# Weights and activations at other places in their buffers, in the second half of a decoder step

## The chip, the cores and the metric

The kernel runs on one core of a Trainium2 chip. The metric is the device time of one execution in microseconds (us). The engines that matter are TensorE (PE in the profile: matmuls; PEld: the loads of its stationary operand, which overlap the matmuls), ScalarE (ACT), VectorE (DVE), GpSimd (POOL) and SyncE (SP, which issues the DMAs).

## The reference

One layer of a hybrid decoder is computed for 288 tokens at once: 256 of a prompt and 8 times 4 of a sample group, all in float32.

```
h = RMSNorm(x); P = h @ w_in            # conv branch, attention branch, memory branch, gates
x = x + (g_A*y_A + g_B*y_B + g_M*y_M) @ w_o
x = x + relu(RMSNorm(x) @ w_up)^2 @ w_down
```

`D_MODEL` is 2048 and the hidden width of the feed-forward part is 8192. The last two lines are the part of the kernel that the change touches: the output projection `w_o`, and the feed-forward part `w_up`, `w_down`.

## The kernel before

All activations lie transposed in SBUF: 128 features in the partitions, 288 tokens along the free axis. A float32 product is made of three fast ones. Both operands are split in a high part (a cast to float32r) and a low part (what the cast left over), and high*high, high*low and low*high are summed in PSUM.

**Weights** arrive in 504 slabs of 128 x 1024 floats, eight blocks of 128 x 128 side by side. SP loads a slab into one of four `wr` buffers (`load_slab`, L285). ACT casts it into a `wh` buffer (`cast_weights`, L303), DVE subtracts and writes the low part to a `wl` buffer (`sub_part`, L314). There are four `wh` and four `wl` buffers.

**Matmuls.** `main_tile` makes one output tile of 128 features x 288 tokens from two slabs; `products` issues 24 matmuls for each slab, all through `chunk` (L486): sixteen with blocks of `wh` as the stationary operand, and the high and low activations in turn as the moving one, then eight with blocks of `wl` and the high activations. Every one of these 24 loads new weights (128 columns) and streams 288 columns.

**Places.** The split activations of the first half, and `h2`, which feeds `w_up`, are `Acts`: two `a` buffers of 320 floats, used from float `AHEAD` = 12 on. The merged branches, which feed `w_o`, and the squared hidden tiles, which feed `w_down`, are `Home`s: places in the `k4` and `s` buffers, which are free by then (`make_homes`). Three of them lie in one `k4` buffer, 320 floats apart, one in an `s` buffer, each also 12 floats in. In the built program all `wr`, `wh`, `wl`, `a`, `k4` and `s` buffers start 96 bytes past a multiple of 256 bytes, so the weights of these matmuls start at 96 and the activations at 144 past such a multiple.

**Order.** All instructions are put in order when the program is built: `Order.run` keeps a list of jobs with estimated costs and pool counts, and takes the one that can start first. Tiles come from pools that turn round; a pool's size is known to this planner. For the second half, `main` issues 16 tiles of `w_o` (32 slabs), and then, four times, 16 tiles of `w_up` and 16 of `w_down` (64 slabs each time): 288 slabs in all, the last ones of the 504.

Of the kernel before, what the change touches and what calls it, by code (L numbers as in the profile page):

```python
# [8 lines left out]
F32R = mybir.dt.float32r  # L9
# [5 lines left out]
P = 128  # L15
D_MODEL = 2048
KT = D_MODEL // P
# [4 lines left out]
T = NP + NS  # L22
# [13 lines left out]
SLAB = 8 * P  # L36
N_SLABS = 504
# [37 lines left out]
class Order:  # L75
# [15 lines left out]
    def add(self, gen, rank, at=None):  # L91
        job = Job(gen, rank, self.now.ready if at is None and self.now else at or 0.0)
        self.jobs.append(job)
        was, self.now = self.now, job
        self.step(job)
        self.now = was
# [10 lines left out]
    def give(self, pool, n=1):  # L107
        self.pools[pool] += [self.now.ready] * n
# [45 lines left out]
def dve(n, *flags, **take):  # L154
    return Ask("DVE", 0.18 + n / 920.0, flags, **take)


def act(n, *flags, **take):
    return Ask("ACT", 0.22 + n / 1200.0, flags, **take)


def pool(n, *flags, **take):
    return Ask("POOL", 0.3 + n / 420.0, flags, **take)


def pe(us, *flags, **take):
    return Ask("PE", us, flags, **take)


def sp(*flags, **take):  # L170
    return Ask("SP", 0.45, flags, **take)


APART = 320
AHEAD = 12
VISIT, VISIT_K = 4, 8
MM = 0.131
MM_MEM = 0.226
# [3 lines left out]
def tile_decoder_step(ctx: ExitStack, tc: tile.TileContext, xT, memT, wall, cvec, kmat, ptab,  # L182
# [1 line left out]
                      yT, oK, oV, oCp, oCs, oMK, oMV):  # L184
    nc = tc.nc
    PS = bass.MemoryType.PSUM
    bufs = {"wr": 4, "w": 4, "a": 75, "t": 11, "k4": 9, "s": 8, "pm": 4, "pa": 3, "pl": 1}

    def open_pool(name, n, space=None):
        if space is None:  # L190
# [17 lines left out]
    def tl(p, shape, dt=F32):  # L208
        cnt[0] += 1
        return pools[p].tile(shape, dt, tag=p, name=f"{p}_{cnt[0]}")  # L210

    def bank(p):
        return tl(p, [P, 512])
# [57 lines left out]
    class Slab:  # L271
        def __init__(self, parts):
            self.parts = parts
            self.landed = [Flag() for _ in range(parts)]
            self.split = [Flag() for _ in range(parts)]
# [4 lines left out]
    def load_slab(s, part):  # L280
# [4 lines left out]
        nc.sync.dma_start(sl.raw[:, part * n:(part + 1) * n], wall[s, :, part * n:(part + 1) * n])  # L285
        sl.landed[part].at = order.landed(n * P * 4 / 1e3)

    def due(s):
        return at_slab[1] + 2.9 * (s - at_slab[0])

# [2 lines left out]
    def cast_weights():  # L293
        todo = [(0, 0), (1, 0), (0, 1), (1, 1)] + [(s, i) for s in range(2, N_SLABS) for i in range(slabs[s].parts)]
        for s, i in todo:
            sl = slabs[s]
            n = SLAB // sl.parts
            cast_at[0] = s
            yield act(n, sl.landed[i], **({} if i else {"w": 1}))
            if i == 0:  # L300
                sl.h = tl("wh", [P, SLAB], F32R)
            c = slice(i * n, (i + 1) * n)
            nc.scalar.copy(sl.h[:, c], sl.raw[:, c])  # L303
            sl.split[i].cast = order.now.ready
            add(sub_part(s, i), lambda s=s: 0 if due(s) - order.free["DVE"] < 5.0 else 4.5)

    def sub_part(s, i):
        sl = slabs[s]
        n = SLAB // sl.parts
        yield dve(n, late=Order.HOP + 0.1)  # L310
        if i == 0:
            sl.l = tl("wl", [P, SLAB], F32R)
        c = slice(i * n, (i + 1) * n)
        nc.vector.tensor_sub(sl.l[:, c], sl.raw[:, c], sl.h[:, c].bitcast(F32))  # L314
        done(sl.split[i])
        if i == sl.parts - 1:
            give("wr")
# [5 lines left out]
    class Acts:  # L323


        def __init__(self, n=T):
            c = slice(AHEAD, AHEAD + n) if n == T else slice(0, n)
            self.h, self.l = tl("a", [P, APART], F32R)[:, c], tl("a", [P, APART], F32R)[:, c]
# [178 lines left out]
    def main_tile(acts, evac, rank=1.0, n_slabs=2):  # L507
        yield pe(0.0, pm=1)
        ps = bank("pm")[:, :T]
        for i in range(n_slabs):  # L510
            slab_no[0] += 1
            yield from products(ps, FULL, acts[8 * i:8 * i + 8], i == 0, i == n_slabs - 1)
            give("w")
        add(evac(ps), rank)
# [720 lines left out]
    homes, homes_in = [], Flag()  # L1235
# [4 lines left out]

    def make_homes():
        yield sp(*conv_done, *osb_in, k4=bufs["k4"], s=bufs["s"])
        parts = []
        for _ in range(bufs["k4"]):
            x = tl("k4", [P, 1024], F32R)
            parts += [x[:, AHEAD + i * APART:AHEAD + i * APART + T] for i in range(3)]
        for _ in range(bufs["s"]):
            parts.append(tl("s", [P, 512], F32R)[:, AHEAD:AHEAD + T])
        for j in range(KT):
            homes.append(Home(parts[2 * j], parts[2 * j + 1]))  # L1250
        done(homes_in)


# [12 lines left out]
    merged = [None] * KT  # L1266

    def branch(br, j):
        def evac(ps):
            sig = gates[br, j]  # L1270
            if br == 2:
                yield dve(T, sig.flag, a=1)
                macc[j] = tl("a", [P, T])
                nc.vector.tensor_mul(macc[j], ps, sig.out)
                give("pm")
                give("t")
                return
            yield dve(T, sig.flag)
            nc.vector.tensor_mul(sig.out, ps, sig.out)
            give("pm")  # L1280
            yield dve(T)
            nc.vector.tensor_add(macc[j], macc[j], sig.out)
            give("t")
            if br == 0:
                yield act(T, homes_in)
                a = merged[j] = homes[j]
                nc.scalar.copy(a.h, macc[j])
                yield dve(T)
                nc.vector.tensor_sub(a.l, macc[j], a.h.bitcast(F32))
                give("a")  # L1290
                done(merged_in[j])
        return evac
# [41 lines left out]
        return load, evac  # L1334


    def up_tile(u, f):
        def evac(ps):
            yield dve(T, r2_done, t=1)
            r = tl("t", [P, T])  # L1340
            nc.vector.scalar_tensor_tensor(r, ps, 0.0, r2, op0=ALU.max, op1=ALU.mult)  # L1341
            give("pm")
            yield pool(T)
            nc.gpsimd.tensor_mul(r, r, r)  # L1344
            yield act(T)
            a = homes[f]
            nc.scalar.copy(a.h, r)  # L1347
            yield dve(T)
            nc.vector.tensor_sub(a.l, r, a.h.bitcast(F32))  # L1349
            give("t")  # L1350
            u[f].h, u[f].l = a.h, a.l
            done(u[f].flag)
        return evac
# [48 lines left out]
    def warm_up():  # L1402

        yield pe(4.2, pa=1)
        junk = bank("pa")
        for i in range(7):
            nc.tensor.matmul(junk, warm[:, :P], warm[:, :512], start=True, stop=True)  # L1407
        give("pa")
        give("w")

    def main():
        yield from warm_up()
        yield from mem_products()
        yield from conv_products([evac_lin(0, "pa"), evac_gat(0, "pa"), evac_lin(1, "pm"), evac_gat(1, "pm")])
        for j in range(2, CT):
            yield from main_tile(hx, evac_lin(j, "pm"))
            yield from main_tile(hx, evac_gat(j, "pm"))
        add(samples(), 3.0)
        for h in range(MH):
            yield from main_tile(hx, mem_head(h), 2 + 0.05 * h)  # L1420
        for h in range(SH):
            yield from main_tile(hx, sb_key(h), 2.2 + 0.05 * h)
            yield from main_tile(hx, sb_query(h), 2.2 + 0.05 * h)
            yield from main_tile(hx, sb_head(h), 2.2 + 0.05 * h)
        yield from branch_products(2, [Late(omem, h, om_in[h]) for h in range(MH)])
        give("a", 8)
        yield from branch_products(1, [Late(osb, h, osb_in[h]) for h in range(SH)])
        give("a", 16)
        yield from branch_products(0, [Late(cact, j, cact_flags[j]) for j in range(CT)])
        give("a", 40)  # L1430
        mg = [Late(merged, j, merged_in[j]) for j in range(KT)]
        for j in range(KT):
            load, evac = out_tile(j)
            add(load(), 2)
            yield from main_tile(mg, evac)
        add(sum_norm(sq_sum, D_MODEL, r2, r2_done, sums_2), 0.4)
        hh = [Late(h2, j, h2_in[j]) for j in range(KT)]
        for c in range(D_FF // D_MODEL):
            u = [Later() for _ in range(KT)]
            for f in range(KT):  # L1440
                yield from main_tile(hh, up_tile(u, f))
            for j in range(KT):
                yield from main_tile(u, down_tile(j, c == D_FF // D_MODEL - 1))

# [174 lines left out]
```

## Time and profile before

| what | value |
|---|---|
| time, median of 2 runs | 1639.87 us (1639.81 to 1639.92) |
| the profiled execution's own time | 1639.37 us |
| its span | 1637.6 us |
| PE busy | 1633.0 us, 12786 instructions |
| DVE busy | 992.2 us |
| ACT busy | 739.3 us |
| POOL busy | 138.9 us |
| mean DMA rate over the span | 186 GB/s |

The span runs from the first to the last instruction of the program; 1.8 us of the execution lie around it. Busy times of the engines overlap. A matmul's record lasts longer than the distance to the next one, since matmuls are pipelined: the rate of PE is read from starts and counts, not from the length of a record.

### The profile page before, as it was taken

To read this page: it belongs to the slowest core of one execution; us is meant where nothing else is said; L and a number is where in the kernel's file an instruction comes from. 1 tells how busy PE (TensorE), PEld (TensorE's weight loads), DVE (VectorE), ACT (ScalarE), POOL (GpSimd) and SP (SyncE) were. 2 spreads that over 40 slices of the span, in tenths; PEclk is the share of its full clock that TensorE was granted. 3 is DMA by queue.
4 is the path that set the end of the run, shared out by engine and by line. 5 is a ranking of instruction groups with operands and counts; after the bars stand their busy time and mean duration, and the time that the engine had idled before them with its cause. 6 is when DMAs were issued, how large, how long until landed. Compare 5 with 4: busy or idle time off the path is not lost.

```text
span 1637.6 us, 30963 instructions
## 1 busy us (share of the span) xinstructions
PE 1633.0 (100%) x12786; PEld 1615.7 (99%) x12786; DVE 992.2 (61%) x1471; ACT 739.3 (45%) x1070; POOL 138.9 (8%) x105
## 2 busy tenths in 40 slices
PE   9999999999999999999999999999999999999999
PEld 7999999999999999999999999999999999999999
DVE  8888888877777655565555544455445554455443
ACT  8746666644343534444443433333333333333332
POOL 0020000000000000001222200122001210022100
PEclk9999999999999999999999999999999999999999
DMA  9686465776755555556655555555555555555563
GB/s 339 217 184 248 148 203 195 251 257 243 256 162 167 152 184 174 169 162 202 193 175 167 170 169 173 170 168 170 167 169 168 169 173 170 169 168 168 179 192 100
DMA packets 107103, 305.39 MB, mean 186 GB/s; under 512 B 19922, under 2 KB 29522, under 8 KB 106962
## 3 DMA queue, kind: packets, MB, share of 16 engines
q1 hardware_dynamic: 106818, 303.39, 58.4%
q8 instruction: 100, 1.64, 0.4%
q14 instruction: 41, 0.34, 0.1%
q10 hardware_dynamic: 144, 0.02, 0.0%
HBM read 297.05 MB, written 6.32 MB: 185 GB/s over the span
## 4 chain that ended last, share of the span: by engine, by line
PE 100%; POOL 0%; DVE 0%; issue 0%; POOLq 0%
PE pm L486 93%; PE pm L539 3%; PE pa L486 1%; PE pl L1015 1%; PE pl L1188 0%; PE pa L852 0%; PE pa L853 0%; PE pa L851 0%; PE pl L1031 0%; PE pa L1407 0%; PE pa L825 0%; PE pa L1142 0%; PE pa L906 0%; PE pa L1139 0%; PE pa L1141 0%; PE pa L1106 0%
## 5 line engine op out<-in xcount | busy, mean ns | idle before, releaser
L303 ACT CAST wh<-wr 128x1024 fp32r<-128x1024 f32 (+1 forms) x520 | 530.5, 1023 | 652.1 <-PE pm L486 596.2
L486 PE MATMUL pm<-a,wh 128*128 128x288 f32 x5184 | 742.3, 293 | 0.0
L314 DVE TENSOR_TENSOR wl<-wr,wh 128x1024 fp32r<-128x1024 f32 (+1 forms) x520 | 616.6, 1189 | 197.2 <-ACT wh L303 192.4
L486 PEld LDWEIGHTS pm<-a,wh 128*128 128x128 f32 x5184 | 699.7, 188 | 1.3 <-issue 1.2
L486 PE MATMUL pm<-a,wl 128*128 128x288 f32 x2592 | 398.6, 293 | 0.0
L486 PEld LDWEIGHTS pm<-a,wl 128*128 128x128 f32 x2592 | 359.8, 188 | 0.0
L486 PE MATMUL pm<-k,wh 128*128 128x288 f32 x2160 | 306.8, 292 | 0.0
L486 PEld LDWEIGHTS pm<-k,wh 128*128 128x128 f32 x2160 | 290.2, 188 | 0.0
L486 PE MATMUL pm<-k,wl 128*128 128x288 f32 x1120 | 171.6, 292 | 0.0
L486 PEld LDWEIGHTS pm<-k,wl 128*128 128x128 f32 x1120 | 155.0, 188 | 0.0
L1344 POOL TENSOR_TENSOR t<-t 128x288 f32<-128x288 f32 x64 | 96.3, 1505 | 599.9 <-DVE t L1341 599.9
L1358 DVE TENSOR_TENSOR a<-a,pm 128x288 f32<-128x288 f32 x64 | 29.1, 454 | 122.5 <-PE pm L486 122.5
L1341 DVE SCALAR_TENSOR_TENSOR t<-pm,r 128x288 f32<-128x288 f32 x64 | 29.2, 458 | 90.3 <-PE pm L486 90.3
L1347 ACT CAST k<-t 128x288 fp32r<-128x288 f32 x56 | 24.2, 433 | 115.7 <-POOL t L1344 115.7
L1260 DVE TENSOR_TENSOR t<-pm,rx 128x288 f32<-128x288 f32 x48 | 22.0, 458 | 73.2 <-PE pm L486 73.2
L486 PE MATMUL pm<-s,wh 128*128 128x288 f32 x400 | 65.0, 293 | 0.0
L717 DVE SCALAR_TENSOR_TENSOR a<-a,cv,a 128x256 f32<-128x256 f32 x120 | 57.7, 481 | 1.4
L1330 POOL TENSOR_TENSOR t<-t,t 128x288 f32<-128x288 f32 x15 | 22.0, 1469 | 420.9 <-ACT t L1327 420.9
L486 PEld LDWEIGHTS pm<-s,wh 128*128 128x128 f32 x400 | 56.6, 188 | 0.0
L1349 DVE TENSOR_TENSOR k<-t,k 128x288 fp32r<-128x288 f32 x52 | 23.8, 458 | 51.1 <-ACT k L1347 51.1
L539 PE MATMUL pm<-wh,a 128*128 128x512 f32 x128 | 35.1, 396 | 0.0
L486 PE MATMUL pm<-s,wl 128*128 128x288 f32 x160 | 33.8, 293 | 0.0
(214 smaller groups left out, 785.5 us busy)
## 6 DMA issues: line engine op xcount, KB each, us to landing
wr<-in_wall SPq DMA_DIRECT2D x488, 512.0 KB, 3.6
wr<-in_wall SPq DMA_DIRECT2D x32, 256.0 KB, 4.8
k<-in_kpool SPq DMA_DIRECT2D x32, 256.0 KB, 6.0
k<-in_vpool SPq DMA_DIRECT2D x32, 256.0 KB, 5.9
k<-in_mkc SPq DMA_DIRECT2D x8, 512.0 KB, 8.8
k<-in_mvc SPq DMA_DIRECT2D x8, 512.0 KB, 6.4
t<-in_xT SPq DMA_DIRECT2D x16, 144.0 KB, 3.6
out_yT<-a SPq DMA_DIRECT2D x16, 144.0 KB, 1.8
```

The lines of the kernel that those rows point to most:

```text
L303: nc.scalar.copy(sl.h[:, c], sl.raw[:, c])
L314: nc.vector.tensor_sub(sl.l[:, c], sl.raw[:, c], sl.h[:, c].bitcast(F32))
L486: nc.tensor.matmul(ps, w, a, start=(first and i == 0), stop=(last and i == len(todo) - 1))
L539: nc.tensor.matmul(ps[m], y[:, m * P:(m + 1) * P], z[:, w], start=(k == 0 and j < 2), stop=(k == KT - 1 and j in (4, 5)))
L717: nc.vector.scalar_tensor_tensor(c[:, :NP], up[:, k:k + NP], w, c[:, :NP], op0=ALU.mult, op1=ALU.add)
L1260: nc.vector.tensor_mul(g, ps, rx)
L1330: nc.gpsimd.tensor_add(sq_sum[0], sq_sum[0], res[0])
L1341: nc.vector.scalar_tensor_tensor(r, ps, 0.0, r2, op0=ALU.max, op1=ALU.mult)
L1344: nc.gpsimd.tensor_mul(r, r, r)
L1347: nc.scalar.copy(a.h, r)
L1349: nc.vector.tensor_sub(a.l, r, a.h.bitcast(F32))
L1358: nc.vector.tensor_add(x1[j], x1[j], ps)
```

## The change

Each of the last 288 slabs gets its own place for the high and for the low part: the `wh` and `wl` tiles become 64 floats longer, and the 1024 floats in use start 0 to 63 floats in, as a table `SHIFT` of drawn numbers says. In most of the table the numbers are multiples of 4 floats (16 bytes). For the third and fourth round of `w_up` they are each of 0 to 63 once, that is, steps of one float (4 bytes). For 192 slabs both parts have the same shift; for `w_down` of the first round, `w_up` of the second, and `w_down` of the fourth they are drawn apart.

The homes get five sets of places: 0 floats in for the merged branches, and 0, 4, 8 and 12 floats in for the hidden tiles of the four rounds. `Acts` keep their 12.

To make room, the `a` pool has 73 buffers and not 75. All buffers still start 96 bytes past a multiple of 256 bytes, the longer ones too, since 64 floats are 256 bytes.

```
+PLACES = (0, 0, 4, 8, 12)
+SHIFT = (
+    (48, 48), (60, 60), (40, 40), (52, 52), (0, 0), (12, 12), (8, 8), (48, 48), (36, 36), (16, 16), (8, 8), (36, 36),
...
+    (26, 26), (54, 54), (29, 29), (44, 44), (16, 44), (24, 12), (36, 40), (16, 40), (60, 16), (12, 0), (20, 48), (40, 8),
...
-    bufs = {"wr": 4, "w": 4, "a": 75, "t": 11, "k4": 9, "s": 8, "pm": 4, "pa": 3, "pl": 1}
+    bufs = {"wr": 4, "w": 4, "a": 73, "t": 11, "k4": 9, "s": 8, "pm": 4, "pa": 3, "pl": 1}
...
+    def shifted(p, s, x):
+        n = SHIFT[s - N_SLABS + len(SHIFT)][x] if s >= N_SLABS - len(SHIFT) else 0
+        return tl(p, [P, SLAB + 64], F32R)[:, n:n + SLAB]
...
-                sl.h = tl("wh", [P, SLAB], F32R)
+                sl.h = shifted("wh", s, 0)
...
-            sl.l = tl("wl", [P, SLAB], F32R)
+            sl.l = shifted("wl", s, 1)
...
+        big = [tl("k4", [P, 1024], F32R) for _ in range(bufs["k4"])]
+        small = [tl("s", [P, 512], F32R) for _ in range(bufs["s"])]
+        for n in PLACES:
+            parts = [x[:, i * APART + n:i * APART + n + T] for x in big for i in range(3)] + [x[:, n:n + T] for x in small]
+            homes.append([Home(parts[2 * j], parts[2 * j + 1]) for j in range(KT)])
...
-                a = merged[j] = homes[j]
+                a = merged[j] = homes[0][j]
...
-    def up_tile(u, f):
+    def up_tile(u, f, c):
...
-            a = homes[f]
+            a = homes[1 + c][f]
...
-                yield from main_tile(hh, up_tile(u, f))
+                yield from main_tile(hh, up_tile(u, f, c))
```

More of the change, by code (lines that the diff above doesn't have):

```diff
@@ L175 @@
 AHEAD = 12
+PLACES = (0, 0, 4, 8, 12)
+SHIFT = (
[24 rows of a table added]
+)
 VISIT, VISIT_K = 4, 8
@@ L1242, in make_homes @@
         yield sp(*conv_done, *osb_in, k4=bufs["k4"], s=bufs["s"])
[L1243 to L1250, printed above, removed]
+        big = [tl("k4", [P, 1024], F32R) for _ in range(bufs["k4"])]
[3 more added lines that the diff above has]
+            homes.append([Home(parts[2 * j], parts[2 * j + 1]) for j in range(KT)])
         done(homes_in)
```

22 rows, old and new, of the table SHIFT are left out of this document.

## The prediction

> **What bounds the kernel now.** I read the page's busy times first, then the chain that ended last. (Columns of a group: busy us, mean ns of one, idle us before.)
>
> ```profile
> span 1637.6 us, 30963 instructions
> PE 1633.0 (100%) x12786; PEld 1615.7 (99%) x12786; DVE 992.2 (61%) x1471; ACT 739.3 (45%) x1070; POOL 138.9 (8%) x105
> ...
> PE 100%; POOL 0%; DVE 0%; issue 0%; POOLq 0%
> PE pm L486 93%; PE pm L539 3%; PE pa L486 1%; PE pl L1015 1%; PE pl L1188 0%; PE pa L852 0%; PE pa L853 0%; PE pa L851 0%; PE pl L1031 0%; PE pa L1407 0%; PE pa L825 0%; PE pa L1142 0%; PE pa L906 0%; PE pa L1139 0%; PE pa L1141 0%; PE pa L
> ```
>
> TensorE never rests, and 93% of the chain is one line, the matmuls of `chunk`. So the time is a count of matmuls times the distance from one start to the next. Next come the busy times of L486 alone in three stretches: before the change's part, between, and the whole part (`w_o`, `w_up`, `w_down`).
>
> ```profile
> core 0: us, PE busy (x) PEld busy (x), PEclk, DMA share, GB/s
> 440.00:540.00 100.00, 99.90 (x755) 99.80 (x755) 1.00 0.53 162
> 550.00:735.30 185.30, 185.30 (x1428) 185.30 (x1427) 1.00 0.54 169
> 735.40:1634.40 899.00, 898.86 (x6914) 898.53 (x6912) 1.00 0.55 171
> ```
>
> The changed part has 288 slabs x 24 = 6912 matmuls in 899.0 us, so 130.0 ns each, the clock granted in full (1.00). The first stretch is slower: 132.3 ns a record. The timeline of PE shows the two rates without other work between; the wh row, the wl row and the next row's start are one slab:
>
> ```profile
> 541.56 2.28 PE L486 MATMUL pm<-a,wh 128*128 128x288 f32 x16
> 543.68 1.22 PE L486 MATMUL pm<-a,wl 128*128 128x288 f32 x8
> 544.74 1.76 PE L486 MATMUL pm<-a,wh 128*128 128x288 f32 x12
> 546.34 0.30 PE L441 MATMUL pa<-t,ones_r 128*128 128x288 f32 x1
> 546.47 0.30 PE L442 MATMUL pa<-t,ones_r 128*128 128x288 f32 x1
> ...
> 847.96 2.24 PE L486 MATMUL pm<-a,wh 128*128 128x288 f32 x16
> 850.04 1.20 PE L486 MATMUL pm<-a,wl 128*128 128x288 f32 x8
> 851.08 2.24 PE L486 MATMUL pm<-a,wh 128*128 128x288 f32 x16
> ```
>
> (544.74 - 541.56) / 24 = 132.5 ns; (851.08 - 847.96) / 24 = 130.0 ns. Same form, same kinds of buffers, same places (weights at 96, activations at 144 past a multiple of 256 bytes). So something finer than the count sets the rate, and with unchanged places it has two values.
>
> **What a place could cost.** Call distance the start of the weights less the start of the activations, modulo 256 bytes; in L486 it is 96 - 144, that is 208. The trace has one other distance in quantity: L539 and L851 to L853 take both operands from the start of their buffers (96 and 96), distance 0.
>
> ```profile
> 20.44 1.07 PE L539 MATMUL pm<-wh,a 128*128 128x512 f32 x4
> ...
> 29.96 1.07 PE L539 MATMUL pm<-wh,a 128*128 128x512 f32 x4
> ...
> 180.43 0.28 PE L851 MATMUL pa<-a,a 128*128 128x256 f32 x1
> ...
> 181.14 1.09 PE L486 MATMUL pm<-a,wh 128*128 128x288 f32 x7
> ```
>
> Between the L539 rows stand seven turns of 4 + 2 matmuls: 9.52 us / 42 = 226.7 ns for 512 columns. Between the last two rows stand six of 256 columns: 0.71 us / 6 = 118.3 ns. Their difference gives 108.4 / 256 = 0.423 ns a column, so 288 columns at distance 0 come to 118.3 + 32 x 0.423 = 131.9 ns. Columns alone would be 288 x 0.423 = 121.9 ns; what is left over is 8.1 ns in the changed part, 10.0 ns at distance 0 and 10.6 ns in the slower rate. That leftover is all that a place can save; it is not all that a place can cost.
>
> **The change part by part.**
>
> *Weights at other places, activations of `w_o` and `w_down` at other places.* Counts and shapes stay: 6912 matmuls, 6912 loads. What changes is the distance. In the changed program, 288 of the 6912 keep 208; the others spread over the sixteen 16-byte distances with 288 to 472 each, and 1152 (48 slabs with odd shifts) lie between those. No row shows such a mixture. The near bounds are the two rates of the same form, 130.0 and 132.5 ns, with distance 0 (131.9) between them. The far bounds: no leftover at all, 121.9 ns, which is -8.1 x 6912 = -56 us; and a load that could not run beside the matmul before it at all: a load's record is 188 ns (groups of the changed part, below), +58 x 6912 = +401 us. I take 131.9 ns, the row measured at another distance than the present one, as the mean of the mixture: +1.9 x 6912 = **+13.1 us**.
>
> [...]
>
> [...]
>
> *Casts and subtractions into shifted buffers.* 288 of each, unchanged in size.
>
> ```profile
> L314 DVE TENSOR_TENSOR wl<-wr,wh 128x1024 fp32r<-128x1024 f32 x286 | 349.6, 1223 | 149.0 <-ACT wh L303 147.5 <-ACT t L1327 1.5
> ...
> L303 ACT CAST wh<-wr 128x1024 fp32r<-128x1024 f32 x285 | 299.2, 1050 | 407.3 <-PE pm L486 381.4 <-issue 25.9
> ...
> L486 PEld LDWEIGHTS pm<-k,wh 128*128 128x128 f32 x2160 | 290.2, 188 | 0.0
> ```
>
> All instructions by stage (before the part; `w_up` of the first round; `w_down` of the first round):
>
> ```profile
> core 0: us, PE busy (x) PEld busy (x) DVE busy (x) ACT busy (x) POOL busy (x), PEclk, DMA share, GB/s
> 440.00:540.00 100.00, 100.00 (x757) 100.00 (x757) 74.93 (x126) 40.40 (x52) 0.00 (x0) 1.00 0.53 162
> ...
> 835.20:935.00 99.80, 99.80 (x770) 99.80 (x769) 54.17 (x68) 41.74 (x54) 23.83 (x16) 1.00 0.56 169
> 935.30:1035.00 99.70, 99.70 (x769) 99.70 (x768) 45.52 (x49) 33.77 (x34) 1.51 (x1) 1.00 0.56 170
> ```
>
> A slab lasts 24 x 130.0 = 3.12 us on PE; a cast is 1.05 us and a subtraction 1.22 us, and the casts wait 381 us for PE to free a buffer. If a shifted write took twice as long, L314 would be 2.44 us a slab and with 0.5 us a slab of other DVE work (54.17 us for 32 slabs, less 1.22 each) 2.9 us, still under the 3.12 us. So 0. With that cover gone PE would wait for each slab what DVE needs above 3.12 us. The loads from HBM keep their buffers, their order and their queue (SP's order is the same, instruction for instruction), so 0 there too. POOL's order is the same.
>
> *73 `a` buffers.* The planner moves work only between some 400 and 560 us: a few conv and gate operations on DVE and ACT change places, and the two pairs L441/L442 of the conv norm come 72 and 96 matmuls earlier on PE. No instruction is added. The second pair stands exactly where the slower rate ends (rows at 546.34). If the rate changes earlier with it: -96 x 2.5 ns = -0.2 us. If it does not change there, the 185.3 us stretch after it keeps 132.5: 1428 x 2.5 ns = +3.6 us. I take 0 and keep both ends. A wait on an `a` buffer would show as PE idle; DVE, which frees them, had a quarter of its time left there (74.93 of 100 us), so none is expected.
>
> **Sum.** Against the profiled execution's 1639.4 us: 1639.4 + 13.1 = 1652.5 us. The median of the runs is 0.5 us above the profiled one, so **1653 us**, +0.8%.
>
> **The rivals.**
>
> *Places don't matter.* Then 130.0 ns stays, and only the rate in the first half can move: 1639.7 to 1643.5 us. For it: the stages by `w_up`, with activations in `a`, and by `w_down`, with activations in `k` and `s` buffers, have one rate (rows from 835.20 and 935.30: 770 and 769 records). Against it: both have distance 208, so they can't speak.
>
> *Some places cost less.* If the mixture's leftover is half of today's, 4 ns, the mean is 126.0 ns: -28 us, 1612 us. For it: the leftover isn't fixed, since one form shows 130.0 and 132.5. Against it: no stretch of L486 is under 130.0 ns, and the only other distance is above. For over 2% (33 us) the leftover must fall under 3.4 ns.
>
> [...]
>
> **How the numbers follow.** Forecast (mean of 130.5 to 134.5 ns, +3 to +31 us): 0.55. Places don't matter: 0.13. Cheaper places, under 2%: 0.07; over 2%: 0.03. Stalling places, over 2%: 0.22. About 2%, 33 us, is what a measurement of this kernel can tell from no change; so faster 0.03, within 0.75, slower 0.22. The range reaches from 1632 (-1.1 ns, past the end of "don't matter" into the cheaper places) to 1690 us (+7.3 ns, past the two stalled distances); the far bounds are left out with some 0.17.
>
> **What would show it.** In the profile after, L486 in the changed part should come to 910 to 915 us for 6912 matmuls, with rates that differ from slab to slab by a few ns, constant within the high or low blocks of a slab. [...] The stage between 550 and 735 us should stay at 130.0 ns, or show 132.5. PE's idle time should stay near zero, and casts should still wait for PE. The prediction is wrong if the mean rate leaves 130.5 to 134.5 ns, or if DVE's L314 becomes what PE waits for.

## The result, and the profile after

The changed kernel takes 1661.25 us (1660.3 to 1662.2), before 1639.87: a ratio of 1.0131, with the 95% interval [1.0114, 1.0147]. The profiled execution has a span of 1658.5 us, 20.9 us over that of before.

The page's busy times after. In the changed code `chunk` is L517, the evacuation of the branches L1302 (L1274 before).

```profile
span 1658.5 us, 30968 instructions
PE 1650.7 (100%) x12786; PEld 1632.9 (98%) x12786; DVE 992.7 (60%) x1471; ACT 738.8 (45%) x1070; POOL 138.7 (8%) x105
```

The counts are the same, and so are the busy times of DVE, ACT and POOL to within 0.5 us; PE has 17.7 us more. The busy time of L517 by stretch shows where:

```profile
core 0: us, PE busy (x) PEld busy (x), PEclk, DMA share, GB/s
460.40:516.00 55.60, 55.60 (x428) 55.60 (x428) 1.00 0.52 155
536.30:741.30 205.00, 205.00 (x1548) 205.00 (x1549) 1.00 0.53 166
741.40:1655.30 913.90, 913.79 (x6913) 913.45 (x6912) 1.00 0.54 168
```

The changed part takes 913.9 us for 6912 matmuls, 132.2 ns each, where before it took 899.0: **+14.9 us**. It begins at 741.4 us, not at 735.4: **+6.0 us ahead of it**. These 6.0 us have two reasons. The stretch from 536 us on runs at 132.4 ns (205.0 us / 1548) where it ran at 130.0; and PE is stopped once, which it never was there before. (From 460 to 516 us the new rate is the better one: 55.6 us / 428 is 129.9 ns, where before had 132.5; that gives back about 1 us.) From the waits of PE (total us, times, longest):

```profile
PE pm L517 <- DVE a L1302: 3.3, 1, 3.3
```

and from the timeline of all engines around it:

```profile
456.41 0.68 PE L517 MATMUL pm<-a,wl 128*128 128x288 f32 x4
457.28 2.56 DVE L748 SCALAR_TENSOR_TENSOR a<-a,cv,a 128x256 f32<-128x256 f32 x5
459.87 0.46 DVE L1302 TENSOR_TENSOR a<-pm,t 128x288 f32<-128x288 f32 x1
...
460.38 1.31 PE L517 MATMUL pm<-a,wh 128*128 128x288 f32 x8 [3.29 <-DVE a L1302]
```

Before, the same evacuation (L1274) stood between two steps of the convolution (L717), and PE did not wait:

```profile
454.37 0.49 DVE L717 SCALAR_TENSOR_TENSOR a<-a,cv,a 128x256 f32<-128x256 f32 x1
454.77 0.46 DVE L1274 TENSOR_TENSOR a<-pm,t 128x288 f32<-128x288 f32 x1
455.14 0.48 DVE L717 SCALAR_TENSOR_TENSOR a<-a,cv,a 128x256 f32<-128x256 f32 x1
```

The evacuation takes a result out of a `pm` bank into an `a` buffer. With 73 of them it stands in DVE's queue behind the last five steps of a convolution tile (L748, 2.56 us), whose end gives a buffer back, and PE waits 3.29 us for the bank.

PE's timeline inside the changed part shows rates that go with the slab's place. Distance is the start of the weights less that of the activations, modulo 256 bytes: 112 in the two slabs from 871.91 us, 128 in that from 884.53, 48 in that from 887.73.

```profile
871.91 2.25 PE L517 MATMUL pm<-a,wh 128*128 128x288 f32 x16
...
875.03 2.24 PE L517 MATMUL pm<-a,wh 128*128 128x288 f32 x16
...
878.15 2.29 PE L517 MATMUL pm<-a,wh 128*128 128x288 f32 x16
...
884.53 2.30 PE L517 MATMUL pm<-a,wh 128*128 128x288 f32 x16
...
887.73 2.30 PE L517 MATMUL pm<-a,wh 128*128 128x288 f32 x16
889.86 1.23 PE L517 MATMUL pm<-a,wl 128*128 128x288 f32 x8
890.92 0.30 PE L517 MATMUL pm<-a,wh 128*128 128x288 f32 x1
```

Start to start a slab of 24 takes 3.12 us at distance 112 (130.0 ns), 3.20 at 128 and 3.19 at 48 (133.3 and 132.9 ns). Worked out from the starts of all 6912 matmuls, the first two and the last of each slab's high block (the 16 with `wh`) and low block (the 8 with `wl`) left out, this is the mean rate in ns by distance:

| distance | 0 | 16 | 32 | 48 | 64 | 80 | 96 | 112 | 128 | 144 | 160 | 176 | 192 | 208 | 224 | 240 |
|---|---|---|---|---|---|---|---|---|---|---|---|---|---|---|---|---|
| activations at 112 or 144 | 131.6 | 131.8 | 131.5 | 133.3 | 132.4 | 131.7 | 132.7 | 130.2 | 133.0 | 133.8 | 130.3 | 131.1 | 132.5 | 130.6 | 132.6 | 131.4 |
| activations at 96 or 128 | 131.5 | 132.0 | 133.2 | 131.7 | 133.3 | 132.4 | 133.2 | 132.1 | 133.3 | 130.8 | 131.6 | 132.7 | 131.9 | 132.3 | 133.4 | 132.3 |

112, 160 and 208 are the cheap distances for activations 16 bytes past a multiple of 32 (130.2, 130.3 and 130.6 ns), and no mean is under 130.0 ns. The two rows differ by up to 3 ns at one distance (133.8 and 130.8 at 144), so where the activations stand counts too. The slowest of the 576 blocks, at distance 60, has 136.1 ns. Where the weights moved in steps of 4 bytes, the places that are no multiple of 16 bytes have 132.4 ns and the others of the same two stages 132.3.

### The profile page after: what moved, and what is told of

The parts are those of the page before. It is cut to its first block, busy times and chain, and to the rows that moved or that the text cites. A ratio compares the mean times of both kernels' runs of the same rounds, so it can differ in the third digit from the quotient of the medians.

```text
span 1658.5 us, 30968 instructions
## 1 busy us (share of the span) xinstructions
PE 1650.7 (100%) x12786; PEld 1632.9 (98%) x12786; DVE 992.7 (60%) x1471; ACT 738.8 (45%) x1070; POOL 138.7 (8%) x105
## 4 chain that ended last, share of the span: by engine, by line
PE 99%; DVE 0%; ACT 0%; issue 0%; POOL 0%; POOLq 0%
PE pm L517 92%; PE pm L570 3%; PE pa L517 1%; PE pl L1046 1%; PE pl L1219 0%; PE pa L883 0%; PE pa L884 0%; PE pa L882 0%; PE pl L1062 0%; PE pa L1435 0%; PE pa L856 0%; DVE a L748 0%; PE pa L1173 0%; PE pa L937 0%; PE pa L1170 0%
## 5 line engine op out<-in xcount | busy, mean ns | idle before, releaser
L517 PE MATMUL pm<-a,wh 128*128 128x288 f32 x5184 | 748.5, 295 | 3.3 <-DVE a L1302 3.3
L517 PEld LDWEIGHTS pm<-a,wh 128*128 128x128 f32 x5184 | 705.6, 188 | 4.8 <-DVE a L1302 3.5
L517 PE MATMUL pm<-a,wl 128*128 128x288 f32 x2592 | 401.5, 294 | 0.0
L517 PEld LDWEIGHTS pm<-a,wl 128*128 128x128 f32 x2592 | 362.5, 188 | 0.0
L517 PE MATMUL pm<-k,wh 128*128 128x288 f32 x2160 | 311.6, 295 | 0.0
L517 PEld LDWEIGHTS pm<-k,wh 128*128 128x128 f32 x2160 | 294.5, 188 | 0.0
L517 PE MATMUL pm<-k,wl 128*128 128x288 f32 x1120 | 174.0, 294 | 0.0
L517 PEld LDWEIGHTS pm<-k,wl 128*128 128x128 f32 x1120 | 157.0, 188 | 0.0
L517 PE MATMUL pm<-s,wh 128*128 128x288 f32 x400 | 65.8, 294 | 0.0
L748 DVE SCALAR_TENSOR_TENSOR a<-a,cv,a 128x256 f32<-128x256 f32 x120 | 57.7, 480 | 1.6
L517 PEld LDWEIGHTS pm<-s,wh 128*128 128x128 f32 x400 | 57.4, 188 | 0.0
L517 PE MATMUL pm<-s,wl 128*128 128x288 f32 x160 | 34.1, 295 | 0.0
```

Of the source, the lines that this page charges most:

```text
L517: nc.tensor.matmul(ps, w, a, start=(first and i == 0), stop=(last and i == len(todo) - 1))
L748: nc.vector.scalar_tensor_tensor(c[:, :NP], up[:, k:k + NP], w, c[:, :NP], op0=ALU.mult, op1=ALU.add)
```

## The experiments

Theory A after this reading: the distance sets the rate, 15 us; the smaller pool costs the 6 us ahead. Rivals: the moved buffers; the activations' own place; the step from one place to the next.

**The smaller pool alone.**

```
-    bufs = {"wr": 4, "w": 4, "a": 75, "t": 11, "k4": 9, "s": 8, "pm": 4, "pa": 3, "pl": 1}
+    bufs = {"wr": 4, "w": 4, "a": 73, "t": 11, "k4": 9, "s": 8, "pm": 4, "pa": 3, "pl": 1}
```

> The kernel before with 73 activation buffers and nothing else; all places stay (distance 208). Theory A (the smaller pool makes the loss ahead of the changed part): PE is again stopped for some 3.3 us near 456 us by an evacuation into an a buffer, and the rate between 536 and 735 us is again 132.5 ns, so the changed part begins about 6 us later than before, and the time is 1645 to 1648 us (the upper end if the slower rate lasts through the output projection). Rival (the moved buffers or the longer weight tiles make it): no stop, 1639 to 1641 us.

Measured: 1662.37 us (1659.6 to 1666.2), ratio 1.0130 [1.0113, 1.0147]. The pool alone costs as much as the whole change. L486 by stretch, then PE's timeline at the stop:

```profile
540.00:744.80 204.80, 204.80 (x1548) 204.80 (x1547) 1.00 0.53 166
744.90:1661.20 916.30, 916.16 (x6914) 915.82 (x6912) 1.00 0.55 167
```

```profile
460.67 2.29 PE L486 MATMUL pm<-a,wh 128*128 128x288 f32 x8 [3.29 <-DVE a L1274]
462.76 1.16 PE L486 MATMUL pm<-a,wl 128*128 128x288 f32 x4
463.72 3.46 PE L486 MATMUL pm<-a,wh 128*128 128x288 f32 x16
```

The stop is there, as theory A said. What no expectation had: the slower rate, once in, lasts to the end, 132.5 ns for all 6912 matmuls with every place unchanged (916.2 us). And after the stop eight matmuls take 2.1 us, 261 ns each. The busy times there give the clock:

```profile
core 0: us, PE busy (x) PEld busy (x) DVE busy (x) ACT busy (x) POOL busy (x), PEclk, DMA share, GB/s
456.00:460.00 4.00, 1.38 (x11) 1.15 (x9) 3.44 (x6) 0.39 (x1) 0.00 (x0) 0.94 0.58 183
460.00:462.00 2.00, 1.33 (x5) 1.33 (x6) 1.83 (x5) 0.00 (x0) 0.00 (x0) 0.50 0.28 113
462.00:464.00 2.00, 2.00 (x11) 2.00 (x10) 0.97 (x4) 0.96 (x1) 0.00 (x0) 0.50 0.00 0
464.00:466.00 2.00, 2.00 (x10) 2.00 (x10) 1.96 (x4) 0.09 (x1) 0.00 (x0) 0.50 0.04 8
466.00:470.00 4.00, 4.00 (x31) 4.00 (x30) 2.09 (x3) 1.05 (x1) 0.00 (x0) 0.96 0.46 131
```

The granted clock is halved (0.50) from the stop to 466.3 us. Behind the restart at 460.67 us that is 5.7 us at half speed, 2.8 us of lost matmuls; in the profile of the changed kernel the same stop left the clock at 1.00. So in this execution the changed part begins 9.5 us late (744.9 against 735.4 us) and takes 17.3 us more (916.3 against 899.0). The profiled execution is the slowest of the four, and the clock does not explain their spread, two near 1660 and two near 1665: the mean granted clock is 0.998 in the profiled one and 0.999 in the other three, of 1659.6, 1659.92 and 1664.82 us. What differed between those three is open. Behind one and the same stop of 3.29 us the clock stays halved for 6.8 us in this profile, for 3.4 us in that of the run with drawn weights alone (next), and not at all in that of the changed kernel; what sets the length, no run shows.

So theory A gets a second half: distance 208 has two lasting rates, and the smaller pool's order leaves the stream in the slower one. In all the profiles with distance 208 ahead of the changed part, the stretch from 548 to 730 us runs at 132.5 ns with 73 buffers (four kernels) and at 130.0 ns with 75 (five).

**Weights alone, homes alone.** The changed kernel with `PLACES = (12, 12, 12, 12, 12)`, and with the shift always 0:

```
-PLACES = (0, 0, 4, 8, 12)
+PLACES = (12, 12, 12, 12, 12)
```

> The changed kernel with all homes at 12 floats again, so that only the weights' places are drawn. Theory A (the distance between weights and activations sets the rate, and a mixture of distances gives some 132.2 ns wherever the activations stand): 132.0 to 132.4 ns in all nine stages of the changed part, +14 to +16 us there, 1659 to 1662 us. [...]

```
-        n = SHIFT[s - N_SLABS + len(SHIFT)][x] if s >= N_SLABS - len(SHIFT) else 0
+        n = 0
```

> The changed kernel with all weight shifts zero, so that only the homes are moved: one distance in each stage. Theory A (a map of rates over distance, read from the profile after): output projection and first w_down (distance 0) 131.7 ns, second w_down (240) 131.7, third (224) 133.3, fourth and all w_up (208) 130.0 or 132.5; +6.5 us in these stages, +6 us ahead of them, so 1651 to 1655 us. Rival (the change from slab to slab costs, not the distance): every stage back at 130.0 ns, 1645 us.

Measured: 1662.14 us with the weights alone (ratio 1.0134 [1.0114, 1.0154]), 1661.97 us with the homes alone (1.0133 [1.0113, 1.0153]). In both profiles the clock was halved behind the stop (0.60 and 0.55 from 462 to 464 and 464 to 466 us with the weights alone, 0.50 from 460 to 466 us with the homes alone), as with the smaller pool alone, which is in these totals; the rates by stage are not touched by it. With drawn weights the nine stages run at 131.7 to 132.5 ns, wherever the homes stand (expected: 132.0 to 132.4), so the activations' own place is no large term in such a mean. The homes alone were expected at 1651 to 1655 us: the rates were in the map, but the sum took 130.0 ns for the stages at distance 208, and four of these five ran at 132.3 to 132.5. L517 by stage with the homes alone (`w_o`; then, behind the first round, the second `w_up` and `w_down` and the third `w_up` and `w_down`):

```profile
744.75:845.00 100.25, 100.25 (x763) 100.25 (x763) 1.00 0.62 191
...
1049.00:1150.00 101.00, 101.00 (x764) 101.00 (x763) 1.00 0.54 166
1150.50:1251.00 100.50, 100.50 (x765) 100.50 (x764) 1.00 0.55 168
1251.50:1351.00 99.50, 99.50 (x767) 99.50 (x766) 1.00 0.55 169
1351.50:1453.50 102.00, 102.00 (x767) 102.00 (x766) 1.00 0.54 165
```

From start to start, 131.7 ns for `w_o` (distance 0), 132.5 for the second `w_up` (1049), 131.7 for the second `w_down` (240), 130.0 for the third `w_up` (1251) and 133.3 for the third `w_down` (224). Two `w_up` stages with the same weights' and activations' places have 132.5 and 130.0 ns: distance 208 has two rates, and something other than these places decides. The rival, that only the step from place to place costs, falls with the 133.3 ns of a whole stage at one distance.

**Places alone, at 75 buffers.** The room comes from constants kept once instead of twice; the same with no shift is the control.

```
-    ones = cpool.tile([P, P], F32, name="ones")
...
-    r2 = cpool.tile([P, T], F32, name="r2")
+    r2 = rx
...
-    bufs = {"wr": 4, "w": 4, "a": 73, "t": 11, "k4": 9, "s": 8, "pm": 4, "pa": 3, "pl": 1}
+    bufs = {"wr": 4, "w": 4, "a": 75, "t": 11, "k4": 9, "s": 8, "pm": 4, "pa": 3, "pl": 1}
```

> The changed kernel with 75 activation buffers; the room for the longer weight tiles comes from two constants that are kept once instead of twice. Theory A (drawn places give a mean of 132.2 ns by themselves): no stop near 456 us, the changed part begins near 735 us and takes 912 to 915 us, 1653 to 1657 us. Rival B (the loss is the smaller pool's, whose order leaves the matmuls in the slower of two rates, and the places cost nothing of their own): changed part at 130.0 ns, 1639 to 1642 us.

> The kernel before with the longer weight tiles and the constants of the run with 75 buffers and drawn places, all places unchanged (distance 208). Theory A: nothing that sets a rate is changed, 130.0 ns in the changed part, 1639 to 1642 us. Rival (the length or address of the weight tiles costs): 132 ns or more there, 1655 us or more.

Measured: 1652.15 us, ratio 1.0076 [1.0059, 1.0092], 0.9 us under the expected range; the control 1637.04 us, 0.9982 [0.9972, 0.9992]. Busy times of `chunk` in the run with drawn places, then in the control:

```profile
545.50:733.30 187.80, 187.80 (x1447) 187.80 (x1446) 1.00 0.55 169
733.40:1647.20 913.80, 913.70 (x6913) 913.40 (x6912) 1.00 0.56 168
```

```profile
441.00:522.00 81.00, 81.00 (x625) 81.00 (x624) 1.00 0.56 165
550.00:733.90 183.90, 183.90 (x1417) 183.90 (x1416) 1.00 0.56 170
734.00:1632.90 898.90, 898.79 (x6913) 898.51 (x6912) 1.00 0.56 171
```

913.8 us again for the changed part, without a stop and from a stretch ahead at 130.0 ns: the places cost 15 us by themselves. Rival B falls. Block by block the mean rates are those of the changed kernel: 568 of the 576 agree within 0.3 ns, though one stream comes in at 130.0 ns and the other at 132.5; the eight others stand at the start of the part and right behind a pair of sums. So the drawn places set their own rates, whichever of the two they meet.

The control was 2.9 us faster than before, where 1639 to 1642 us were expected. In the profiles it is 1.4 us (spans of 1636.2 and 1637.6 us): from 441 to 522 us the control runs at 130.0 ns where the kernel before runs at 132.5, 625 records against 614:

```profile
441.00:522.00 81.00, 81.00 (x614) 81.00 (x613) 1.00 0.53 163
```

**One other distance for all.** 160 bytes left free ahead of the weight buffers make it 112, 96 bytes make it 48; 112 was also run with 73 buffers.

```
+    open_pool("pad", 1).tile([P, 40], F32, name="pad")
     pools["wh"] = open_pool("wh", bufs["w"])
```

> The kernel before (75 buffers, 12 floats) with 160 bytes left free ahead of the weight buffers: distance 112 in place of 208 for every matmul of the kernel. Theory A (the rate is a function of the distance, and 112 has only the rate of 130.0 ns, where 208 has 130.0 and 132.5): changed part 130.0 ns as before, the stretches ahead of it that run at 132.5 ns go to 130.0, which saves 3 to 8 us: 1632 to 1637 us. Rival (the slower rate comes from other work running beside, or from a state that any distance can fall into): the same stretches stay at 132.5 ns, 1639 to 1641 us.

> The kernel before with 73 activation buffers and distance 112 for all matmuls. Theory A (the smaller pool costs 3.3 us by the stop near 456 us, and the rest of its 22 us only because distance 208 has a second rate of 132.5 ns into which the matmuls fall there; 112 has no such rate): changed part 130.0 ns, 1640 to 1644 us. Rival (73 buffers slow the matmuls whatever the distance): 132 ns or more in the changed part, 1655 to 1662 us.

> The kernel before with 96 bytes left free ahead of the weight buffers: distance 48 for every matmul. Theory A (rate by distance; slabs at 48 ran at 133.3 ns in the profile after): 133.3 ns throughout, +23 us in the changed part and some +8 us ahead of it, 1665 to 1674 us. Rival (a constant distance is never slow for long, and only the change from one to another costs): 130.0 ns, 1637 to 1641 us.

Measured: 1637.89 us at 112 (ratio 0.9986 [0.9976, 0.9995]), 1648.61 us at 112 with 73 buffers (1.0046 [1.0029, 1.0062]), 1673.92 us at 48 (1.0208 [1.0187, 1.0228]). `chunk` by stretch at 48 and, in the second fence, at 112 with 73 buffers:

```profile
540.00:747.10 207.10, 207.00 (x1553) 206.90 (x1552) 1.00 0.55 166
747.20:1669.10 921.90, 921.80 (x6913) 921.48 (x6911) 1.00 0.55 166
```

```profile
739.95:842.00 102.05, 102.05 (x788) 102.05 (x787) 1.00 0.62 193
850.00:1645.60 795.60, 795.60 (x6069) 795.44 (x6067) 1.00 0.55 166
```

48 holds 133.3 ns from 540 us to the end. The 1632 to 1637 us that were expected at 112 were missed by 1 us: from 441 to 515 us the stream runs at 131.1 ns from start to start there, and not at 130.0. At 112 with the smaller pool `w_o` runs at 130.0 and the feed-forward part at 131.1 ns (795.6 us / 6069): the second rate again, nearer to the first than at 208. The expected 1640 to 1644 us was missed by this and by the clock, which was halved after the stop in this profile as well (0.50 from 460 to 464 us). Here too the clock does not order the runs: the one whose mean clock is 1.000 took 1647.91 us, one with 0.999 took 1644.91. The rival's 132 ns did not come.

**What switches the rate.** Two more matmuls ahead of every fourth output tile of the feed-forward part, at 208 and at 112, and a version at 112 with the constants kept once:

```
+    def apart(i):
+        if i % 4 == 0:
+            yield pe(2 * MM, h2_in[0], pa=1)
+            total(h2[0].h, h2[0].l, T)
+            give("pa")
...
             for f in range(KT):
+                yield from apart(f)
                 yield from main_tile(hh, up_tile(u, f, c))
```

> The kernel before (75 buffers, distance 208) with two more matmuls, whose sums nobody reads, ahead of every fourth output tile of the feed-forward part: 64 matmuls, 8.3 us at 130 ns. Theory A (the rate is a state of TensorE's own stream, and any break in the stream can change it): among the 32 stretches between the pairs some run at 130.0 and some at 132.5 ns, 1650 to 1662 us. Rival (the slower rate comes from what ACT and DVE do beside, which is unchanged): all 32 at 130.0 ns, 1648 us.

> The same added pairs at distance 112. Theory A (112 has the rates 130.0 and 131.1 ns): the 32 stretches take only these two, 1646 to 1653 us. Rival (132.5 ns is open to every distance): some stretches at 132.5 ns, up to 1660 us.

> A version meant to beat both kernels: 75 buffers, the two constants kept once, places of before but distance 112. Theory A: changed part at 130.0 ns; ahead of it no stretch over 131.1 ns, where distance 208 still has some at 132.5: 1633 to 1638 us. Rival (the state after each break is drawn anew, and 131.1 can last): up to 1645 us.

Measured: 1648.95 us (ratio 1.0054 [1.0034, 1.0075]) and 1646.63 us (1.0040 [1.0024, 1.0056]); from start to start, all 31 whole stretches between pairs run at 130.0 ns at both distances. At 208 theory A had some at 132.5 and missed, and its rival, the work of ACT and DVE, fits; but equal pairs, met in the same state, are one case and not 32. At 112 the first pair did switch the stream: the 59 matmuls behind it run at 131.1 ns, until the pair of sums at 842 us sets it back. The third run was meant to beat both kernels and did not: 1644.77 us, 1.0030 [1.0019, 1.0041], the upper end that its rival gave. It has 130.0 ns until the pair of sums at 842 us, and 131.1 ns to the end (789.7 us / 6024). It has 75 buffers, so the same drop with 73 at 112 can't be put down to the pool alone:

```profile
734.00:841.00 107.00, 107.00 (x825) 107.00 (x824) 1.00 0.63 192
850.00:1639.70 789.70, 789.70 (x6024) 789.53 (x6022) 1.00 0.55 167
```

So the last run has pairs that differ in their place:

```
+            n = 4 * (pairs[0] % 8)
+            pairs[0] += 1
+            ss = bank("pa")[:, :256]
+            nc.tensor.matmul(ss, ones_r, h2[0].h[:, n:n + 256], start=True, stop=False)
+            nc.tensor.matmul(ss, ones_r, h2[0].l[:, n:n + 256], start=False, stop=True)
```

> The kernel before with the added pairs, but of 256 columns, and from one pair to the next their activations start 16 bytes further (eight places in turn, four times), so that the breaks in the stream differ; the 32 equal pairs switched nothing. Theory A (the rate is a state of the stream that a break can switch, depending on the break's places): some of the 32 stretches at 132.5 ns, and the same ones when the eight places come again from the same state; 1648 to 1660 us. Rival (no break between running matmuls switches the rate): all 32 at 130.0 ns, 1647 us.

Measured: 1657.70 us, ratio 1.0107 [1.0077, 1.0136]. PE's timeline around one pair:

```profile
1165.81 1.59 PE L486 MATMUL pm<-k,wh 128*128 128x288 f32 x11
...
1168.93 0.28 PE L1408 MATMUL pa<-a,ones_r 128*128 128x256 f32 x1
1169.05 0.28 PE L1409 MATMUL pa<-a,ones_r 128*128 128x256 f32 x1
...
1172.35 1.63 PE L486 MATMUL pm<-k,wh 128*128 128x288 f32 x11
...
1175.53 0.70 PE L486 MATMUL pm<-k,wh 128*128 128x288 f32 x4
```

3.12 us for the slab ahead of the pair, 3.18 us for the second one behind it: 130.0, then 132.5 ns. Of 31 whole stretches 19 run at 132.5 and 12 at 130.0 ns, none between, and the thirteen behind pairs 4 to 16 repeat behind pairs 20 to 32, rate for rate. The rate is a state of the matmul stream, and a break of two matmuls can switch it. Places alone don't tell which break does: they come again every eight pairs, but behind pair 4 the rate is 130.0 and behind pair 12 it is 132.5 ns. The repeat after sixteen speaks for the state that the break meets as the other part. It is not the work of ACT and DVE beside: stretches of `w_up` (23.5 us hold 183 matmuls from 914 us on and 180 from 1245.5 us on) and of `w_down` (3.18 us a slab behind the pair at 1168.93 us, 3.12 behind that at 1194.60) are found at both rates.

## Why the prediction was right, and where it was not

**The mixture of distances** was the step that carried the forecast: 131.9 ns, +13.1 us. Measured: 132.2 ns, +14.9 us, and the run with 75 buffers shows that this is the places' own cost. The anchor held as well: a stage at distance 0 ran at 131.7 ns where the two widths of L539 and L851 gave 131.9. That this one distance could stand for the mean of sixteen was luck: the means of the table go from 130.2 to 133.8 ns, and distance 0 happens to lie near the middle. A row at 112 (130.0 ns) or at 48 (133.3) in its place would have given 0 or +23 us.

**Places don't matter** (0.13) fell: with 75 buffers the drawn places cost 15 us, and 48 costs 34 us in the whole kernel. With nothing changed but the room left free ahead of the weight buffers, the part runs at 130.0 ns at distance 112 and at 133.3 at 48. **Cheaper places** fell: no distance has a mean under 130.0 ns. **Stalling places** (0.22, and the upper end of the range, +7.3 ns for two stalled distances) fell: that a place stalls was the author's guess, and no run shows a distance that does. The worst one adds 3.8 ns to 130.0 (133.8 at 144), and the slowest of 576 blocks has 136.1 ns. The far bound of +401 us was too near for what it names: it takes a load's record of 188 ns as the whole step, and an estimate for a load that ran beside nothing is that record and the 121.9 ns of the columns together. Nothing rested on it.

**Odd shifts** show no cost of their own: 132.4 ns for the places that are no multiple of 16 bytes, against 132.3 for the others of the same two stages.

**Casts and subtractions** cost nothing, as said. The groups in the changed part after:

```profile
L345 DVE TENSOR_TENSOR wl<-wr,wh 128x1024 fp32r<-128x1024 f32 x286 | 349.5, 1222 | 151.9 <-ACT wh L334 151.9
...
L334 ACT CAST wh<-wr 128x1024 fp32r<-128x1024 f32 x285 | 298.7, 1048 | 421.0 <-PE pm L517 394.2 <-issue 26.8
```

1222 and 1048 ns an operation, as before (1223 and 1050), and the casts still wait for PE (394.2 us).

**73 buffers** is the step that failed: "a wait on an `a` buffer would show as PE idle ... none is expected", 0, with ends at -0.2 and +3.6 us. Measured +6.0 us ahead of the part: 3.3 us of stop, and some 3.6 us because the slower rate stayed after 536 us (the upper end that was written down), less 1 us from 460 to 516 us, where the rate was 130.0. DVE's quarter of free time said nothing about one moment at which a buffer was missing. Worse than its size is its kind: it was taken as an addend. Alone, the pool costs 22 us, most of it (17.3 of 26.8 us in the profile) because it leaves the stream at 132.5 ns for the whole second half; with the drawn places, which replace that rate by their own 132.2, it costs 9 us (1661.25 against 1652.15, the latter with the constants kept once). Between the two profiles the sum was 7.8 us low: 6.0 us by this step and 1.8 us by the mixture.

## What to carry to other kernels

Where TensorE streams without a gap, as here, 2.5% of its rate can hang on where weights and activations start relative to each other (130.0 ns at distance 112, 133.3 at 48): compare the time from start to start stage by stage, not busy shares. A stream that keeps a slower rate for hundreds of microseconds may have been put there by one small break long before (131.1 ns for 790 us behind the pair of sums at 842 us, at distance 112), so two changes that each touch it don't add up; measure them apart. And a smaller pool does not come free just because its engines have idle time (22 us by itself here): look for the one moment at which its last buffer is wanted.

## What the runs showed that was not expected

Matmuls of one form at one distance have two lasting rates, 130.0 and 132.5 ns at 208, 130.0 and 131.1 ns at 112. At 132.5 ns and 208 the distances from start to start repeat every eight matmuls (140, 135, 131, 131, 133, 127, 133, 130 ns, to within 1 ns), for 800 us on end in the run with the smaller pool. Why there are two rates, why eight, and by what the distance acts on the rate, no run tells. Two runs were faster than the kernel before by 0.1 to 0.2% (1637.04 and 1637.89 us), as far as the profiles show by the rate of a few stretches in the first half; the attempt to join the two ended at 1644.77 us, at 131.1 ns. A stop of 3.3 us can cost nearly twice its length: with the clock halved behind it, another 2.8 us were lost. Right behind the same stop, from 466 to 515 us, the four kernels with 73 buffers and distance 208 run at 130.0, 132.5, 132.5 and 130.1 ns; why, no run tells.
